# Holding small matmuls to the dense chunk ahead of them, in a two-layer hybrid encoder

## The chip, the cores and the metric

The kernel runs on one core of a Trainium2 chip. The metric is the time of one execution on the device, in microseconds (us): the median of three runs, with the lowest and the highest beside it. The engines of the core are TensorE (PE, with its weight loads listed apart as PEld), VectorE (DVE), ScalarE (ACT), GpSimd (POOL) and SyncE (SP). SP, ACT and POOL also issue DMA transfers.

## The reference

The model is an encoder of two layers over 1040 positions (16 learned ones in front of 1024) with 1024 channels, in float32. In each layer:

- `h = h + hybrid_mixer(rmsnorm(h))`, where one projection gives q, k, v (4 heads of 128, each through a 3-tap convolution and SiLU), a gate z, the coefficients beta and decay, and the three parts B, C, h of a gated short convolution of 512 channels.
- q and k are normalised to length 1. A gated delta rule runs over the positions forwards and backwards: in each chunk, with K the keys and G the running sum of the log decays,

```
M = strict_lower(beta * K K^T * exp(G_i - G_j));  A = I + M
u, w = solutions of A u = beta v, A w = beta k exp(G)
attn = q K^T * exp(G_i - G_j)
v_new = u - w S;  o = q exp(G) S + attn v_new;  S = S exp(G_last) + k_dec^T v_new
```

- both directions are added, normalised per head, multiplied by silu(z), joined with the short convolution, projected out and added to h.
- `h = h + swiglu(rmsnorm(h))` with an inner width of 2816 (22 row tiles of 128).

A last RMSNorm follows, and the 16 learned positions are dropped.

## The kernel before

Activations lie with channels on the partitions: a row is one tile of 128 channels by 1040 positions, and a full activation is eight rows. Float32 products are made of three matmuls: every operand is split into a rounded part and the rest (`hi`, `lo`), and a product is hi*hi + hi*lo + lo*hi.

`dense` (lines 142 to 169) makes one output row: for each chunk of about 347 (or 512) positions it takes a PSUM bank, issues 3 matmuls for each of the K rows of the input, hands the bank to an evacuation, and then takes one job from each of three lists, `jobs`, `jobs2`, `jobs3`. This is how the work of the delta rule is put among the dense projections: a slot is one chunk of 24 matmuls, and a `None` in a list is an empty slot.

The order on each engine is not that of the source alone. The program is built with a planner that runs a timeline of its own, and puts on each engine, at each moment of that timeline, the ready instruction with the smallest priority number. Numbers grow in source order, unless `at_prio` sets them: `low` (line 723) gives a job's matmuls a place behind the dense matmuls issued so far. `after(ins, prev)` (line 85) adds a dependency, so that `ins` comes behind `prev`. On the chip each engine then runs its list in that order and waits where something is not there yet.

In each layer the steps are, in the order of the source:

1. Input projection of the k rows, then the q rows (`seq`, line 660), convolution and SiLU. `lengths` and `sums` (lines 624 to 658) square them and sum over the channels with small matmuls (L629) into a bank of their own; `normalise` scales k.
2. From the fourth tile on, `jobs2` gets one `chunk_p` (line 467) per chunk of positions, 9 in all. It makes the key product K K^T (L477) in bank "b", transposes the keys (`k_out`, L448), and for each direction loads the decay sums (L481, issued by ScalarE), forms the exponents (L483 on VectorE, L484 on ScalarE), stores them for later (L485) and multiplies product by exponents into `P` (L487). Eight buffers `ptm` hold exponents.
3. `sub_start` and `substitute` invert the 32-blocks of A on VectorE. `invert(d)` (line 553) joins them to blocks of 128 with matmuls: `first` (L576), `second_third` for each half of the 32 (chunk, head) pairs (L588, L589), and three `fourth_fifth` (L610, L612), each with copies on ScalarE (L579, L593, L594, L616, L618) that the next step needs. Direction 0 uses banks "f", direction 1 banks "b". They are put into `jobs3`, direction 0 when the last v tile begins, direction 1 with the third z tile.
4. v, z and the short convolution follow (`sc_tile`, line 763); `chunk_a` makes the query products (L513). The scan over the chunks runs beside the last of these projections.
5. The output projection takes first the short-convolution rows. Their splits `ys` (L950, L951) lie in buffers that held rows 4 to 7 of the projection's input `x`; the third of these rows is loaded (L945) into a buffer that held the low parts of rows 0 to 3, and the residual rows `hr` (L967) into those of rows 0 to 3.
6. While the output projection ends, `early_part(f, q)` (line 1095) makes parts of the first four gate tiles f: the half q = 0 is made of four input rows in one bank, copied out by ScalarE (L1105), and the half q = 1 goes on adding in the same bank. Its matmuls are those of `prod` (L1065, L1068, L1069), and each call is chained behind the last matmul of the call before by `after`.
7. SwiGLU with a seven-product scheme of block sums, and the down projection.

## Time and profile before

| | |
|---|---|
| median of three runs | 2469.58 us (2468.56 to 2469.79) |
| profiled execution | 2473.65 us, span 2471.9 us |
| PE busy | 2448.0 us (99%), 17530 instructions |
| VectorE busy | 1779.7 us (72%) |
| ScalarE busy | 1057.9 us (43%) |
| GpSimd busy | 67.2 us (3%) |
| mean DMA rate | 136 GB/s |

The profile is of one execution. Its page gives each engine's busy time, the chain of work that ended last, and the costliest groups; other views list who waited for whom, the busy time of stretches, and the instructions in order of time. A line such as `PE pf L610 <- ACT b L616: 1.9, 1, 1.9` says that PE, before an instruction of line 610 that writes a bank "f", stood idle until ScalarE had done line 616: 1.9 us in all, once, at the longest 1.9. "issue" stands for a wait that no recorded event ended. A row of the timeline gives the start and the length in us, the engine, the line, the operation, out<-in, the shapes, and in brackets the idle time before it and what ended that. The ends of matmuls are modelled: one of 346 columns is shown as some 0.33 us long while the next starts 0.16 us after it. PE's busy time is therefore no measure of how well it is fed; its waits are. Layer 0 is the time up to about 1250 us, layer 1 the rest.

### The profile page before, as it was taken

Reading aid. Unit: us, or ns where it says so; the run is one execution under the profiler, and the core shown is the slowest. Engines: PE = TensorE matmul, PEld = TensorE weight load, DVE = VectorE, ACT = ScalarE, POOL = GpSimd, SP = SyncE. Lnnn points to the kernel's source line nnn. Section 1 sums busy time; section 2 is a strip of 40 time slices with the busy share of each in tenths; the row PEclk is TensorE's granted clock in tenths of the full one; section 3 lists DMA queues with packets and bytes.
Section 4 is the critical chain, followed back from the end, with each engine's and each line's share of the span. In section 5 each row is a group of like instructions: output and inputs, shape, how many; then the busy total and the mean of one; then the engine's idle time right before and its main releaser. Section 6 shows DMA issues by size and latency. Waiting matters only on the chain.

```text
span 2471.9 us, 44873 instructions
## 1 busy us (share of the span) xinstructions
PE 2448.0 (99%) x17530; PEld 2259.7 (91%) x17530; DVE 1779.7 (72%) x3296; ACT 1057.9 (43%) x1964; POOL 67.2 (3%) x157
## 2 busy tenths in 40 slices
PE   9999999999999999999999999999999999999998
PEld 8999999999999999999999988998988888888887
DVE  6788445759877777878667984447798777678775
ACT  5654333536333333444446643335453333234544
POOL 0130000000000000000000200000000000000002
PEclk9999999999999999999999999999999999999999
DMA  4445344524323322675224443535342233237641
GB/s 133 149 155 169 121 160 133 200 76 133 114 90 115 117 95 87 196 228 162 87 91 148 163 153 123 164 124 205 120 139 97 91 111 116 88 110 251 209 132 69
DMA packets 201321, 335.26 MB, mean 136 GB/s; under 512 B 23404, under 2 KB 88356, under 8 KB 201108
## 3 DMA queue, kind: packets, MB, share of 16 engines
q1 hardware_dynamic: 172996, 293.83, 35.9%
q10 hardware_dynamic: 25936, 34.19, 4.3%
q0 software_dynamic: 2176, 4.36, 0.6%
q8 instruction: 138, 2.26, 0.4%
q14 instruction: 75, 0.61, 0.1%
HBM read 250.31 MB, written 81.99 MB: 134 GB/s over the span
## 4 chain that ended last, share of the span: by engine, by line
PE 92%; DVE 4%; DMA 2%; ACT 1%; issue 1%; SPq 0%; ACTq 0%; DVEq 0%
PE pacc L153 10%; PE pacc L154 10%; PE pacc L155 10%; PE pacc L1069 4%; PE pacc L1065 4%; PE pacc L1068 4%; PE pb L1065 3%; PE pb L1069 3%; PE pb L1068 3%; PE pf L1065 3%; PE pf L1069 3%; PE pf L1068 3%; PE pacc L1492 2%; PE pacc L1489 2%; PE pacc L1491 2%; PE pa L1065 1%
## 5 line engine op out<-in xcount | busy, mean ns | idle before, releaser
L153 PE MATMUL pacc<-a,whi 128*128 128x346 f32 (+1 forms) x800 | 263.0, 329 | 2.3 <-ACT a L950 1.0
L155 PE MATMUL pacc<-a,wlo 128*128 128x346 f32 (+1 forms) x800 | 261.0, 327 | 0.1
L153 PE MATMUL pacc<-b,whi 128*128 128x346 f32 (+2 forms) x672 | 233.7, 348 | 0.0
L155 PE MATMUL pacc<-b,wlo 128*128 128x346 f32 (+2 forms) x672 | 232.1, 347 | 0.0
L154 PE MATMUL pacc<-a,whi 128*128 128x346 f32 (+1 forms) x681 | 223.9, 329 | 0.9 <-DVE a L174 0.6
L154 PE MATMUL pacc<-b,whi 128*128 128x346 f32 (+2 forms) x580 | 200.4, 346 | 0.0
L126 ACT ACTIVATE whi<-raw 128x512 fp32r<-128x512 f32 x166 | 104.6, 631 | 221.0 <-PE pacc L154 178.7
L153 PEld LDWEIGHTS pacc<-a,whi 128*128 128x128 f32 x800 | 151.8, 190 | 5.8 <-ACT a L950 1.8
L127 DVE TENSOR_TENSOR wlo<-raw,whi 128x512 fp32r<-128x512 f32 x166 | 114.2, 688 | 59.1 <-ACT whi L126 52.5
L155 PEld LDWEIGHTS pacc<-a,wlo 128*128 128x128 f32 x800 | 151.8, 190 | 1.7 <-issue 1.0
L153 PEld LDWEIGHTS pacc<-b,whi 128*128 128x128 f32 x672 | 126.8, 189 | 10.3 <-issue 1.9
L155 PEld LDWEIGHTS pacc<-b,wlo 128*128 128x128 f32 x672 | 126.5, 189 | 9.2 <-issue 1.3
L154 PEld LDWEIGHTS pacc<-a,whi 128*128 128x128 f32 x681 | 129.2, 190 | 5.1 <-issue 2.0
L1047 ACT ACTIVATE whi<-rw 128x512 fp32r<-128x512 f32 x92 | 58.0, 634 | 140.7 <-PE pf L1068 39.4
L154 PEld LDWEIGHTS pacc<-b,whi 128*128 128x128 f32 x580 | 109.3, 188 | 6.9 <-issue 0.4
L1047 ACT ACTIVATE b<-rw 128x512 fp32r<-128x512 f32 x64 | 40.0, 632 | 134.5 <-PE pacc L1068 38.0
L1047 ACT ACTIVATE a<-rw 128x512 fp32r<-128x512 f32 x64 | 40.4, 633 | 93.8 <-PE pacc L1068 59.9
L316 DVE TENSOR_TENSOR a<-pacc,rstd 128x346 f32<-128x346 f32 (+2 forms) x59 | 32.6, 553 | 50.4 <-PE pacc L155 50.3
L316 DVE TENSOR_TENSOR b<-pacc,rstd 128x346 f32<-128x346 f32 (+1 forms) x63 | 32.4, 514 | 47.7 <-PE pacc L155 47.5
L1048 DVE TENSOR_TENSOR wlo<-rw,whi 128x512 fp32r<-128x512 f32 x92 | 62.8, 685 | 3.4 <-ACT whi L1047 3.1
L1065 PE MATMUL pacc<-b,whi 128*128 128x260 f32 (+1 forms) x172 | 52.7, 307 | 0.7 <-ACT b L1105 0.7
L1069 PE MATMUL pacc<-b,wlo 128*128 128x260 f32 (+1 forms) x172 | 52.7, 306 | 0.0
(981 smaller groups left out, 7866.3 us busy)
## 6 DMA issues: line engine op xcount, KB each, us to landing
raw<-in_w_in SPq DMA_DIRECT2D x110, 256.0 KB
raw<-in_w_gu SPq DMA_DIRECT2D x104, 256.0 KB
rw<-in_w_gu SPq DMA_DIRECT2D x88, 256.0 KB
rw<-in_w_dn SPq DMA_DIRECT2D x94, 192.0 KB
rec<-vkd SPq DMA_DIRECT2D x61, 256.0 KB
raw<-in_w_out SPq DMA_DIRECT2D x48, 256.0 KB
b<-ad SPq DMA_DIRECT2D x45, 260.0 KB
a<-ad SPq DMA_DIRECT2D x45, 256.0 KB
```

The source lines that it names most:

```text
L126: whi_done[0] = act(out=hi, in_=raw[:, 0:kk, :], func=AF.Copy)
L127: whi_done[1] = tt(out=lo, in0=raw[:, 0:kk, :], in1=hi.bitcast(F32), op=ALU.subtract)
L153: mm(ps[:, :n], wh, xh[:, n0:n1], start=(k == 0), stop=False)
L154: mm(ps[:, :n], wh, xl[:, n0:n1], start=False, stop=False)
L155: mm(ps[:, :n], wl, xh[:, n0:n1], start=False, stop=(k == K - 1))
L316: tt(out=t[:, n0:n1], in0=ps, in1=rstd[:, n0:n1], op=ALU.mult)
L1047: act(out=hi, in_=src, func=AF.Copy)
L1048: tt(out=lo, in0=src, in1=hi.bitcast(F32), op=ALU.subtract)
L1065: one = mm(ps[:, :CW], w[0][:, k, :], th[:, cs], start=first and k == 0, stop=False, skip_group_check=True)
L1068: mm(ps[:, :CW], w[0][:, k, :], tl[:, cs], start=False, stop=False, skip_group_check=True)
L1069: one = mm(ps[:, :CW], w[1][:, k, :], th[:, cs], start=False, stop=stop and k == nk - 1, skip_group_check=True)
L1489: one = mm(ps[:, :CW], wh[:, k, :], th[:, cs], start=st, stop=False, skip_group_check=True)
```

## The change

`dense` notes the last matmul that it issued in `last_mm`. The first matmul of each key product, of each length sum and of each inverse step (of `first`, only its first half) gets a dependency on the matmul noted at that time: the last one of the chunk that was issued just ahead of the job.

The slots move: direction 0's `invert` begins three slots later and has two empty slots between the two halves of `second_third`. The exponents' part of `chunk_p` becomes `chunk_g`, and the slot of chunk c makes its product and then the exponents of chunk c+1; those of chunk 0 take the slot ahead.

The last projection of the last `sc_tile` uses, in its last chunk, rows 4 to 7 of its input before rows 0 to 3. The order of the early products changes from (0,0) (0,1) (1,0) (1,1) (2,0) (2,1) (3,0) (3,1) to (0,0) (1,0) (0,1) (1,1) (2,0) (3,0) (2,1) (3,1).

```diff
-    def dense(ws, xs, chunks, evac, pool=None):
+    last_mm = [None]
+
+    def dense(ws, xs, chunks, evac, pool=None, order=None):
...
-            for k in range(K):
+            ks = order if order and n1 == L else range(K)
+            for i, k in enumerate(ks):
                 (wh, wl), (xh, xl) = ws[k], xs[k]
-                mm(ps[:, :n], wh, xh[:, n0:n1], start=(k == 0), stop=False)
+                mm(ps[:, :n], wh, xh[:, n0:n1], start=(i == 0), stop=False)
                 mm(ps[:, :n], wh, xl[:, n0:n1], start=False, stop=False)
-                mm(ps[:, :n], wl, xh[:, n0:n1], start=False, stop=(k == K - 1))
+                last_mm[0] = mm(ps[:, :n], wl, xh[:, n0:n1], start=False, stop=(i == K - 1))
...
-        def chunk_p(c):
+        def chunk_g(c):
 
             if not Pd:
...
             n, s0 = span(c)
-            kk = bank("b").rearrange("p (h i) -> p h i", h=4)
-            for h in range(H):
-                end = mm(kk[0:n, h, 0:n], KTt[:, h, s0:s0 + n], KTt[:, h, s0:s0 + n], start=True, stop=True)
-            k_out(c, end)
             for d in (dirs0 if c == 0 else (0, 1)):
                 gr = ptm[(2 * c + d) % 8]
                 adma(gr[0:n, :, 0:n], gd[36 * d + 4 * c:36 * d + 4 * c + 4, 0:n].partition_broadcast(n))
...
                 act(out=gr[0:n, :, 0:n], in_=gr[0:n, :, 0:n], func=AF.Exp, scale=-1.0)
                 adma(dtd[c, d].rearrange("p (h i) -> p h i", h=4)[0:n, :, 0:n], gr[0:n, :, 0:n])
+
+        def chunk_p(c):
+
+            n, s0 = span(c)
+            kk = bank("b").rearrange("p (h i) -> p h i", h=4)
+            for h in range(H):
+                end = mm(kk[0:n, h, 0:n], KTt[:, h, s0:s0 + n], KTt[:, h, s0:s0 + n], start=True, stop=True)
+                if h == 0:
+                    after(end, last_mm[0])
+            k_out(c, end)
+            for d in (dirs0 if c == 0 else (0, 1)):
+                gr = ptm[(2 * c + d) % 8]
                 dst = P0[d] if c == 0 else Pv[d][:, 4 * c - 4:4 * c, :]
                 tt(out=dst, in0=kk[0:n, :, 0:n], in1=gr[0:n, :, 0:n], op=ALU.mult)
...
-                                 for q in range(qs.start, qs.stop) for (f, s) in pairs])
+                                 for q in range(qs.start, qs.stop) for (f, s) in pairs][0], qs.start == 0)
...
-                low(lambda: [turn(q) for q in range(qs.start, qs.stop)])
+                    return one
+
+                low(lambda: [turn(q) for q in range(qs.start, qs.stop)][0], True)
...
-                low(lambda: [turns(i) for i in range(n)])
+                low(lambda: [turns(i) for i in range(n)][0], True)
...
-            return [first] + [lambda qs=qs: second_third(qs) for qs in halves] + [lambda a=a, b=b: fourth_fifth(a, b) for a, b in (((0, 1), ()), ((2, 3), (0, 1)), ((), (2, 3)))]
+            return [first, lambda: second_third(halves[0])] + [None] * (2 - 2 * d) + [lambda: second_third(halves[1])] + [lambda a=a, b=b: fourth_fifth(a, b) for a, b in (((0, 1), ()), ((2, 3), (0, 1)), ((), (2, 3)))]
...
-                mm(l2s[which][32 * j:32 * j + 32, :n1 - n0], sel[:, 3 - q:35 - q], sq_[:, n0:n1], start=(q == 0), stop=(q == 3), skip_group_check=True)
+                one = mm(l2s[which][32 * j:32 * j + 32, :n1 - n0], sel[:, 3 - q:35 - q], sq_[:, n0:n1], start=(q == 0), stop=(q == 3), skip_group_check=True)
+                if j == 0:
+                    after(one, last_mm[0])
...
-                jobs2.extend([None, None] + [lambda c=c: chunk_p(c) for c in range(9)])
+                jobs2.extend([None, lambda: chunk_g(0)])
+                jobs2.extend([lambda c=c: (chunk_p(c), chunk_g(c + 1)) for c in range(8)] + [lambda: chunk_p(8)])
...
-        def low(f):
+        def low(f, hold=False):
 
             here = tc.cur_priority
             at_prio(mmp[0])
-            f()
+            one = f()
+            if hold:
+                after(one, last_mm[0])
...
-                jobs3.extend(invert(0))
+                jobs3.extend([None] * 3 + invert(0))
...
-                inproj(18 + 3 * i, times(t2), chunks=ochunks)
+                inproj(18 + 3 * i, times(t2), chunks=ochunks, order=(4, 5, 6, 7, 0, 1, 2, 3))
...
-            for f, q in {5: [(0, 0)], 6: [(0, 1)], 7: [(1, 0)]}.get(m, ()):
+            for f, q in {5: [(0, 0)], 6: [(1, 0)], 7: [(0, 1)]}.get(m, ()):
...
-        for f, q in ((1, 1), (2, 0), (2, 1), (3, 0), (3, 1)):
+        for f, q in ((1, 1), (2, 0), (3, 0), (2, 1), (3, 1)):
```

More of the change, by code (lines that the diff above doesn't have):

```diff
@@ L308, in trunk, with inproj @@
         ochunks = TAIL if last else FULL
-        def inproj(i, evac, pool=None, chunks=FULL):
+        def inproj(i, evac, pool=None, chunks=FULL, order=None):
             ws = pre.pop(i) if i in pre else wload(w_in[l, i], KT)
-            dense(ws, x, chunks, evac, pool)
+            dense(ws, x, chunks, evac, pool, order)
         def to_row(t):
@@ L586, in turn @@
                 def turn(q):
-                    for (f, s) in pairs:
-                        mm(ps[B[f], q - qs.start, :], QS[B[s], q, :], P_[B[s], q, B[s]], start=True, stop=True, skip_group_check=True)
+                    one = [mm(ps[B[f], q - qs.start, :], QS[B[s], q, :], P_[B[s], q, B[s]], start=True, stop=True, skip_group_check=True) for (f, s) in pairs][0]
                     mm(ps[B[s0], q - qs.start, :], P_[B[s0], q, B[s0]], QS[B[s0], q, :], start=True, stop=True, skip_group_check=True)
-                low(lambda: [turn(q) for q in range(qs.start, qs.stop)])
+                    return one
+                low(lambda: [turn(q) for q in range(qs.start, qs.stop)][0], True)
                 for (f, s) in pairs:
@@ L607, in turns @@
                 def turns(i):
+                    out = []
                     for q in range(8):
                         if q4s:
-                            mm(pss[i][S_, q, :], P_[F_, 8 * q4s[i] + q, S_], X64[F_, 8 * q4s[i] + q, :], start=True, stop=True, skip_group_check=True)
+                            out.append(mm(pss[i][S_, q, :], P_[F_, 8 * q4s[i] + q, S_], X64[F_, 8 * q4s[i] + q, :], start=True, stop=True, skip_group_check=True))
                         if q5s:
-                            mm(pss[i][F_, q, :], X64[S_, 8 * q5s[i] + q, :], P_[S_, 8 * q5s[i] + q, S_], start=True, stop=True, skip_group_check=True)
-                low(lambda: [turns(i) for i in range(n)])
+                            out.append(mm(pss[i][F_, q, :], X64[S_, 8 * q5s[i] + q, :], P_[S_, 8 * q5s[i] + q, S_], start=True, stop=True, skip_group_check=True))
+                    return out[0]
+                low(lambda: [turns(i) for i in range(n)][0], True)
                 for i, q4 in enumerate(q4s):
```

## The prediction

> **What bounds the kernel now.** I read the page first, then the list of what TensorE waited for, then the timeline around each wait.

> ```profile
> span 2471.9 us, 44873 instructions
> ...
> PE 92%; DVE 4%; DMA 2%; ACT 1%; issue 1%; SPq 0%; ACTq 0%; DVEq 0%
> ```

> TensorE (PE) carries 92% of the chain that ended last. What the change can win is time in which PE stands still, and what it can lose is new time of that kind. All of PE's idle stretches that touch the change are in one short list (engine and line, what was waited for, us in total, times, longest):

> ```profile
> PE pf L610 <- ACT b L616: 1.9, 1, 1.9
> PE pf L588 <- issue: 1.8, 1, 1.8
> PE pb L477 <- DVE P L487: 1.5, 1, 1.5
> ...
> PE pacc L153 <- ACT a L950: 1.0, 2, 0.6
> ...
> PE pa L1065 <- ACT c L1105: 0.8, 1, 0.8
> ...
> PE pacc L1065 <- ACT b L1105: 0.7, 1, 0.7
> PE pf L589 <- issue: 0.7, 1, 0.7
> PE pf L1065 <- ACT b L1105: 0.7, 1, 0.7
> ...
> PE pb L1065 <- ACT b L1105: 0.4, 1, 0.4
> ...
> PE pa L448 <- ACT kt L450: 0.4, 1, 0.4
> PE pacc L154 <- DVE a L951: 0.3, 1, 0.3
> ```

> They add up to 10.2 us, 0.4% of the span: that is nearly the whole prize. The rest of the list is of the kernel's first microseconds, its last ones and the first sums, which the change leaves alone. The next rows are stretches, the last of them one dense chunk (window, its length, PE busy and instructions, clock, DMA share, GB/s):

> ```profile
> 210.68:213.70 3.02, 2.34 (x193) 1.00 0.57 180
> 278.24:279.38 1.14, 1.14 (x98) 1.00 0.00 0
> ...
> 237.41:241.31 3.90, 3.90 (x28) 1.00 0.70 242
> ```

> A dense chunk of 24 matmuls takes 3.90 us (the last row; four of its 28 are neighbours). So one slot of the job lists, a chunk, is worth 3.9 us of cover.

> **The change, part by part.** The sum is made against the profiled execution's own time, 2473.65 us (span 2471.9). The three timed runs have a median of 2469.58, 4.1 us lower, and I take the difference over unchanged. 0.2% of it is 4.9 us, about what a measurement can tell from no change.

> *Inverse steps of direction 0.* Their six steps are moved to later slots and each is held behind the last matmul of the chunk ahead of its slot. What each issues goes along: matmuls, ScalarE copies and three VectorE instructions per half, no DMA; nothing passes SyncE's or GpSimd's queue. The steps now:

> ```profile
> 207.74 0.59 ACT L579 ACTIVATE b<-pf 32x512 f32<-32x512 f32 x1
> 208.36 1.19 ACT L579 ACTIVATE b<-pf 32x512 f32<-32x512 f32 x2
> ...
> 216.41 1.14 PE L610 MATMUL pf<-b,P 64*64 64x64 f32 x16
> 217.83 1.14 PE L610 MATMUL pf<-b,P 64*64 64x64 f32 x16
> ...
> 224.05 0.27 PE L610 MATMUL pf<-b,P 64*64 64x64 f32 x1 [1.92 <-ACT b L616]
> ```

> The row at 224.05 is the fifth step put two dense matmuls into a chunk while its ScalarE copy is not there; PE stands for 1.92 us. In the new order that step waits behind the whole chunk, 22 matmuls or 3.6 us further on, and the copy is done. I take −1.9; the ends are 0 (another step is late in its place) and −1.9. The fourth step stands in two pieces around one dense matmul (216.41, 217.83); held, it is one piece. The gap between the pieces is 0.28 us, and with the like in the other direction's first step I take −0.6 (ends 0 and −0.8).

> *The two halves of the second step* are put two slots apart for direction 0. Now they run together, 192 matmuls, and PE stops in the middle:

> ```profile
> 212.06 0.20 PE L588 MATMUL pf<-P,b 32*32 32x32 f32 x2
> 212.94 0.18 PE L589 MATMUL pf<-b,P 32*32 32x32 f32 x1 [0.68 <-issue]
> ...
> q8 instruction: 3, 0.05, 1.4%
> ...
> q8 instruction: 2, 0.03, 1.3%
> ```

> In the stretch table the pair takes 3.02 us; one half of the other direction, alone between chunks, takes 1.14. So 3.02 − 2 × 1.14 = 0.74 us are lost here and 1.8 in layer 1 (the "issue" row), 2.5 in all. The two queue rows are of 205 to 220 us and of 276 to 286: instruction blocks are fetched at both places, and only where two halves consume them at once, with other DMA running (share 0.57), does PE run dry. Whether the halves really come apart depends on when the first is ready:

> ```profile
> 209.48 0.38 PE L513 MATMUL pb<-b,b 128*128 128x128 f32 x2
> ```

> Its copies end at 208.33 (207.74 + 0.59), inside the chunk behind which this row stands, and the second half is held to the end of that same chunk. Ready one chunk earlier they are apart, else they are only some matmuls apart. I take half, −1.2; the ends are 0 and −2.5.

> [...]

> *Early products.* The two halves (q = 0 and 1) of one row tile use the same bank, and the second must wait until ScalarE has copied the first out. Those are the four rows L1065 <- L1105: 0.8 + 0.7 + 0.7 + 0.4 = 2.6 us. In the new order another product (or an out-projection tile) lies between them, 24 matmuls of 0.12 us (rows below) or 2.9 us, longer than any of those waits. The same loads and splits are issued, in another order on SyncE's queue. −2.6; the ends are −2.6 and +0.8, one such wait by a bank now held longer.

> *Length sums and key products.* The query length sums are one job; now its parts run as early as each row is there:

> ```profile
> 127.93 1.08 PE L629 MATMUL pf<-sq,sel 128*32 128x260 f32 x16
> ...
> 153.39 0.65 PE L629 MATMUL pf<-sq,sel 128*32 128x260 f32 x8
> ...
> 1366.44 0.62 PE L629 MATMUL pf<-sq,sel 128*32 128x260 f32 x2
> ...
> 1391.61 0.65 PE L629 MATMUL pf<-sq,sel 128*32 128x260 f32 x8
> ```

> These are the first and the last visit of four in each layer. A visit of 8 takes 0.65 us and one of 16 takes 1.08, so merging two saves 0.22. Held behind the job's chunk, which ends shortly before the fourth visit, the first three merge: 2 × 0.22 in each layer, and some half chunk less broken up; I take −1.0 (ends 0 and −1.5). The key products' hold binds nothing: each is held to a chunk that has long been done when its rows arrive.

> *Decay exponents one slot ahead.* ScalarE's DMA issues (one load and one store for each chunk and direction) and its exponentials move past one chunk's evacuation:

> ```profile
> 82.22 0.24 ACT L484 ACTIVATE ptm<-ptm 16x64 f32<-16x64 f32 x1
> ...
> 94.34 0.64 ACT L484 ACTIVATE ptm<-ptm 128x512 f32<-128x512 f32 x1 [0.46 <-DVE ptm L483]
> 112.75 0.33 ACTq L481 DMA_DIRECT2D ptm<-gd  x1
> ...
> 129.68 1.14 DVE L483 SCALAR_TENSOR_TENSOR ptm<-ptm,nGb,off 128x128 f32<-128x128 f32 x4 [2.04 <-DMA ptm<-gd]
> ```

> Eight exponents, all that the buffers hold, are done by 95 us, long before the products; the ninth load, at 112.75, waits for a buffer that a product frees. So the lead is there already. The 1.5 us (L477 <- L487) come from the last row: VectorE waits 2.04 us for such a load, and the product that frees the bank is behind it. I take 0, with −1.9 (the waits of L477 and L448) and +1.5 (one more such wait) as ends.

> *Late rows.* In the last chunk of the last input projection the rows 4 to 7 are used first. Their buffers, which the rows for the output projection take, come free 12 matmuls earlier, those of rows 0 to 3 later; into the latter go the third row and eight residual loads of 520 KB on SyncE's queue:

> ```profile
> 473.88 0.38 SPq L945 DMA_DIRECT2D a<-yd  x1
> ...
> 477.99 0.86 ACT L950 ACTIVATE a<-b 128x348 fp32r<-128x348 f32 x2
> ...
> 1698.68 0.32 SPq L945 DMA_DIRECT2D b<-yd  x1
> ...
> 1704.25 1.14 ACT L950 ACTIVATE b<-a 128x512 fp32r<-128x512 f32 x2
> ```

> The splits, first at 477.99, can start about 2 us earlier; the third row's load, now at 473.88, then starts at the projection's end, no later than 477.99: at most 4.1 us later, and in layer 1 5.6 (1704.25 − 1698.68). What PE waits there now is 1.0 + 0.3 us. Gain and loss are of one size, so 0; the ends are −1.3 and +9.7 (4.1 + 5.6, with nothing to fill them).

> *The holds themselves.* The early products are chained by such holds already, and the first matmul after one starts on time:

> ```profile
> 601.94 0.29 PE L1069 MATMUL pb<-a,wlo 128*128 128x260 f32 x1
> 602.06 0.28 PE L1065 MATMUL pa<-b,whi 128*128 128x260 f32 x1
> ```

> 0.12 us, the usual step: 0. At worst each of 24 inverse holds waits out the matmul ahead, 0.28 us less the step of 0.12: +3.8.

> Sum: −1.9 − 0.6 − 1.2 − 2.6 − 1.0 = −7.3, so 2466.3 for a profiled execution and 2462.3 for the median.

> **Rivals.**
> 1. *The inverse's waits only move.* ScalarE's copies come as late at the new places and the halves stay together: −1.9 and −1.2 fall away, −4.2 is left, 2465.4, no measurable change. For it: both halves are ready inside one chunk. Against it: direction 1, at such places already, has no wait in the list.
> 2. *The third row is late.* The output projection stands for its load: −7.3 + 9.7 = +2.4, 2472.0, no change. Against it: scan matmuls lie there to fill in.
> 3. *Slower: VectorE stands for the exponents' loads.* Place: the products of chunks 4 to 8 in both layers. Each pair of exponents now follows straight behind the products of the chunk before; where its load is late, VectorE stops, the bank is not freed and PE stops as at L477. Ten chunks at 1.5 us are +15: 2477.3. It decides from 12.2 us in all, 1.2 a chunk. For it: the 2.04 us. Against it: only one of ten shows it now.

> **How the numbers follow.** Forecast 0.60; rival 1 0.16; rival 2 0.08; rival 3 0.16. Faster 0.60, same 0.24, slower 0.16. The time is the forecast's, 2462.3. Its own range goes down to −12.5 with the lower ends of inverse, halves, products and sums (−1.9 − 0.8 − 2.5 − 2.6 − 1.5 = −9.3) and of the other two (−1.9 − 1.3), 2457; I go to 2455 for what PE loses between matmuls and the list does not show. The upper end takes in rivals 1 and 2 and most of rival 3: 2476.

> **What would show it.** In the list of PE's waits: no L610 <- L616, no L1065 <- L1105, and the two "issue" rows gone or shorter; L629 for the queries in two visits instead of four; each inverse step of direction 0 in one piece at a chunk's end. The L950 row tells of the late rows, L477 <- L487 of the exponents. I am wrong if new rows of over 1 us stand in that list, above all L477, or L153 for the third row.

## The result and the profile after

The changed kernel takes 2465.12 us (median of 22 runs), the kernel before 2469.45 us (22 runs beside them). The ratio is 0.9985, with a 95% interval of 0.9978 to 0.9991: 4.3 us or 0.17% faster by the medians, and 0.15% by the ratio, at the edge of what can be told from no change. The runs of one kernel lie within 0.5% of each other, but for one of 7159.99 us (late rows undone, below), which is left out of that kernel's ratio. The profiled execution of the changed kernel took 2464.69 us, its span is 2462.9 us, 9.0 us shorter than the span of before.

In the changed kernel the lines are numbered anew: `dense` is L156 to L158, the key product L491, the products with the exponents L498, the inverse steps L587 to L624, the early products L1083 to L1087 with their weights' splits L1065 (ScalarE) and L1066 (VectorE), the copies out of their bank L1123, the splits of the short-convolution rows L968.

What PE waited for in the changed kernel (engine and line, what was waited for, us in total, times, longest):

```profile
PE pb L491 <- DVE P L498: 1.6, 3, 0.8
PE pa L753 <- ACT b L765: 1.3, 1, 1.3
PE pa L451 <- ACT kt L453: 1.2, 2, 0.8
...
PE pf L1087 <- DVE wlo L1066: 0.7, 1, 0.7
PE pa L1087 <- DVE wlo L1066: 0.7, 1, 0.7
...
PE pf L1083 <- ACT b L1065: 0.6, 1, 0.6
PE pa L1083 <- ACT b L1065: 0.5, 1, 0.5
...
PE pb L1087 <- DVE wlo L1066: 0.4, 1, 0.4
PE pacc L156 <- ACT a L968: 0.2, 1, 0.2
...
PE pa L1087 <- DVE b L1066: 0.2, 1, 0.2
```

The inverse's wait for its own copy and both "issue" rows are gone, as forecast. Gone too are the four waits of the early products for the copies out of their bank; but six waits for the splits of weights (L1065, L1066) stand in their place, 0.7 + 0.7 + 0.6 + 0.5 + 0.4 + 0.2 = 3.1 us against 2.6 before: the two of 0.7 in the early products of layer 0, the other four in layer 1 in the regular products right behind the early ones. The waits for the short-convolution rows, 1.3 us before, are 0.2. A new wait of 1.3 us is that of a transpose (L753) for a copy on ScalarE, in the middle of the inverse.

The list doesn't hold all of the difference. In the trace of before the granted clock falls four times to half, each time for 3.41 us. Two of these stretches, each with the one ahead of it (window, its length, busy time and instructions of PE, PEld, DVE, ACT and POOL, granted clock, DMA share, GB/s):

```profile
478.37:481.78 3.41, 2.29 (x11) 1.43 (x10) 3.41 (x9) 3.41 (x10) 0.00 (x0) 1.00 0.98 370
481.78:485.20 3.42, 3.12 (x12) 2.82 (x12) 3.42 (x9) 3.42 (x12) 0.00 (x0) 0.50 1.03 398
...
1451.17:1454.58 3.41, 1.67 (x158) 1.55 (x148) 3.31 (x11) 1.05 (x1) 0.00 (x0) 1.00 0.46 142
1454.58:1457.99 3.41, 3.39 (x36) 3.33 (x37) 3.27 (x9) 3.30 (x7) 0.00 (x0) 0.50 0.84 244
```

The seventh column is the clock. In the windows ahead PE stood for 1.12 and 1.74 us (the late rows' waits, the "issue" stop of layer 1); in the windows behind, it worked at 0.50 (matmuls of 348 columns start 0.29 us apart there, at 482.84 and 483.13 us, against 0.16 at 1.00), by estimate up to 3.41 × 0.5 = 1.71 us beside the wait itself. What it did cost is less: kernels below that have the same waits and no such fall are 0.7 us shorter over each of the two stretches. The other two falls, at 10.7 and 58.5 us, lie in the first products and sums, of which the change only holds the length sums of the k rows; in the traces below falls at 55 to 58 us come with that hold and without it. In the changed kernel's trace the clock doesn't fall before the last 12 us, where it falls in every trace. At its turn to the output projection:

```profile
470.00:473.40 3.40, 3.40 (x25) 3.40 (x24) 3.40 (x9) 3.40 (x15) 0.00 (x0) 1.00 0.67 200
473.40:476.80 3.40, 3.18 (x19) 2.44 (x18) 3.40 (x10) 2.96 (x11) 0.00 (x0) 1.00 1.02 409
```

The main matmuls (`dense` and the products) are the same in number and order in all these kernels, so the time between the starts of two of them can be compared from trace to trace. In us, for stretches by the count of such matmuls (start: the first 240; keys: up to 720; inverse: up to 1440; turn: 1920 to 2400; early: 2640 to 3120; in layer 1 keys and inverse 8160 to 9600, turn 9840 to 10560, early 10560 to 11040):

| kernel | start | keys 0 | inverse 0 | turn 0 | early 0 | keys, inverse 1 | turn 1 | early 1 |
|---|---|---|---|---|---|---|---|---|
| before | 58.56 | 97.09 | 158.67 | 94.66 | 60.65 | 323.64 | 149.90 | 110.78 |
| changed | 54.35 | 96.12 | 156.91 | 91.91 | 60.63 | 323.07 | 149.30 | 111.08 |
| late rows alone | 54.29 | 95.78 | 156.86 | 91.95 | 60.57 | 322.96 | 149.10 | 111.78 |
| inverse alone | 54.33 | 99.34 | 156.79 | 93.93 | 61.82 | 322.15 | 149.90 | 110.34 |
| late rows undone | 56.19 | 95.06 | 158.46 | 93.94 | 60.66 | 321.79 | 149.96 | 109.83 |
| inverse undone | 54.22 | 96.68 | 165.46 | 91.91 | 62.24 | 325.45 | 149.30 | 111.42 |
| halves together | 56.17 | 95.86 | 160.76 | 91.91 | 63.66 | 324.32 | 149.30 | 112.81 |
| early order undone | 54.33 | 95.67 | 156.91 | 91.91 | 60.42 | 323.26 | 149.29 | 109.87 |
| weights ahead | 54.56 | 95.38 | 156.89 | 93.45 | 61.21 | 323.30 | 149.30 | 111.45 |
| more load buffers | 56.34 | 96.66 | 156.89 | 93.44 | 62.45 | 322.55 | 149.33 | 113.92 |
| keys undone | 57.79 | 96.66 | 156.97 | 93.49 | 60.67 | 321.41 | 149.10 | 111.15 |
| exponents undone | 54.26 | 96.45 | 156.91 | 91.91 | 60.65 | 321.55 | 149.30 | 111.64 |
| early order undone, own bank | 56.32 | 95.46 | 155.99 | 91.91 | 60.62 | 321.79 | 149.10 | 110.04 |

Of the 9.0 us between the two spans 4.2 lie in the start, which is the same work in all of them. It takes 54.2 to 54.6 us in the seven traces without a fall of the clock there, 56.2 to 56.3 in the four with one and 57.8 to 58.6 in the two with two, before among them (in the two kernels made from the kernel before by one edit it takes 54.3). Leaving that out, 4.8 us are left, close to the 4.3 of the medians. The stretches win 6.7 us: 2.75 at the turn of layer 0, 1.76 at the inverse and 0.97 at the keys of layer 0, 0.6 each at the keys and inverse and at the turn of layer 1. They lose 0.3 in the early products of layer 1 and 0.3 in the gate products and the rest, and the trace of the changed kernel is 0.4 us longer ahead of the first main matmul and 0.9 behind the last.

### The profile page after: what moved, and what is told of

Read it like the earlier page. It is cut to its first block, busy times and chain, and to the rows that moved or that the text cites. A ratio compares the mean times of both kernels' runs of the same rounds, so it can differ in the third digit from the quotient of the medians.

```text
span 2462.9 us, 44865 instructions
## 1 busy us (share of the span) xinstructions
PE 2443.2 (99%) x17530; PEld 2256.0 (92%) x17530; DVE 1783.6 (72%) x3296; ACT 1055.9 (43%) x1964; POOL 68.1 (3%) x157
## 5 line engine op out<-in xcount | busy, mean ns | idle before, releaser
L156 PE MATMUL pacc<-a,whi 128*128 128x346 f32 (+1 forms) x800 | 261.8, 328 | 0.4 <-ACT a L968 0.2
L158 PE MATMUL pacc<-a,wlo 128*128 128x346 f32 (+1 forms) x800 | 259.1, 325 | 0.0
L156 PE MATMUL pacc<-b,whi 128*128 128x346 f32 (+2 forms) x672 | 232.9, 347 | 0.0
L158 PE MATMUL pacc<-b,wlo 128*128 128x346 f32 (+2 forms) x672 | 232.0, 347 | 0.0
L156 PEld LDWEIGHTS pacc<-a,whi 128*128 128x128 f32 x800 | 150.8, 189 | 3.6 <-issue 1.1
L158 PEld LDWEIGHTS pacc<-a,wlo 128*128 128x128 f32 x800 | 150.7, 189 | 1.0 <-issue 0.6
L158 PEld LDWEIGHTS pacc<-b,wlo 128*128 128x128 f32 x672 | 126.4, 188 | 10.0 <-issue 1.7
L156 PEld LDWEIGHTS pacc<-b,whi 128*128 128x128 f32 x672 | 126.4, 188 | 9.5 <-issue 1.0
L1065 ACT ACTIVATE whi<-rw 128x512 fp32r<-128x512 f32 x92 | 57.9, 634 | 134.7 <-PE pf L1086 35.8
L1065 ACT ACTIVATE b<-rw 128x512 fp32r<-128x512 f32 x64 | 40.2, 632 | 140.3 <-PE pacc L1086 38.6
L1065 ACT ACTIVATE a<-rw 128x512 fp32r<-128x512 f32 x64 | 40.2, 631 | 102.8 <-PE pacc L1086 62.6
L1066 DVE TENSOR_TENSOR wlo<-rw,whi 128x512 fp32r<-128x512 f32 x92 | 63.0, 686 | 2.9 <-ACT whi L1065 2.2
L1087 PE MATMUL pacc<-b,wlo 128*128 128x260 f32 (+1 forms) x172 | 52.7, 306 | 0.0
```

The costliest lines, as they stand in the source:

```text
L156: mm(ps[:, :n], wh, xh[:, n0:n1], start=(i == 0), stop=False)
L158: last_mm[0] = mm(ps[:, :n], wl, xh[:, n0:n1], start=False, stop=(i == K - 1))
L1065: act(out=hi, in_=src, func=AF.Copy)
L1066: tt(out=lo, in0=src, in1=hi.bitcast(F32), op=ALU.subtract)
L1087: one = mm(ps[:, :CW], w[1][:, k, :], th[:, cs], start=False, stop=stop and k == nk - 1, skip_group_check=True)
```

## Experiments

The kernels were timed in several sessions, with the kernel before beside them in each; its medians there run from 2469.45 to 2472.37 us. So a difference of some 2 us between the medians of two sessions tells nothing. Each kernel also has one trace, and the planner lays out everything behind an edit anew, so a trace can differ in places that the edit doesn't touch.

### The late rows, alone and undone

The first kernel is the kernel before with this edit alone; the second is the changed kernel without it.

```diff
-                inproj(18 + 3 * i, times(t2), chunks=ochunks)
+                inproj(18 + 3 * i, times(t2), chunks=ochunks, order=(4, 5, 6, 7, 0, 1, 2, 3))
```

> The kernel before with the late rows alone (rows 4 to 7 first in the last chunk of the last input projection). Theory C (clock): the two waits of PE at this place (1.0 and 0.3 us) cost more than they last, because in the trace of before the granted clock falls to 0.5 for 3.41 us right behind them, which is 1.71 us more. So the waits and the fall of the clock at 480 us are gone, the stretch of layer 0 is 2 to 3 us shorter, and the median is 2466.5 to 2468. Rival (prediction): 0, 2469.5, a new wait for the third row's load takes the place.

> The changed kernel with rows 0 to 7 in their old order in the last chunk of the last input projection. T: the late rows carry the largest share, 2.75 us in layer 0 and 0.6 in layer 1, so the stretch at the turn to the output projection is longer by that, waits of PE before the out projection for the splits of the short-convolution rows come back (about 1.3 us in the list), and the median is 2468.4. R (the prediction): the part is worth 0, 2465.1; what differs at the turn between the two traces is the order in which scan matmuls fell there.

Alone: 2466.46 us against 2470.95 of before, ratio 0.9986 (0.9978 to 0.9995), 4.5 us faster by the medians. Undone: 2467.10, ratio to before 0.9991 (0.9982 to 1.0000), so 2.0 us over the changed kernel. Of PE's waits with the late rows alone the first two rows are the stops in the second inverse step, the third is the one left at the turn (lines of that kernel; L951 is the split):

```profile
PE pf L589 <- issue: 1.9, 1, 1.9
...
PE pf L590 <- issue: 0.8, 1, 0.8
...
PE pacc L154 <- ACT a L951: 0.5, 1, 0.5
```

and at the turn with the late rows undone:

```profile
PE pacc L156 <- ACT a L968: 1.1, 2, 0.6
...
PE pacc L157 <- DMA rec<-vkd: 0.4, 1, 0.4
```

In the table the turn of layer 0 takes 91.9 us in every kernel with the late rows but three in which it takes 93.4 to 93.5 (in two of these the clock falls at 495 and 501 us with nothing to be seen ahead of it, in the third a scan matmul waits 0.9 us), and 93.9 without them where no fall follows, 94.7 in before where one does. In layer 1 it is 149.1 to 149.3 with and 149.9 to 150.0 without. So the part is worth 2.0 us in layer 0, 2.75 with the fall, and 0.6 to 0.8 in layer 1. The prediction's 0 is out. The clock theory forecast the size, but not for the reason it gave: 2.0 of the 2.75 us are there in traces without the fall, and the fall itself is worth 0.7. Most of the 2.0 are the waits themselves, which the list shows too short. Its idle time begins at the modelled end of the matmul ahead, some 0.33 us behind that one's start, while the next matmul could have started 0.16 us behind it; three waits of 1.4 us in the list so become some 2 us, against some 0.4 left with the late rows. In layer 1 what goes is a wait of a scan matmul for VectorE (L842), which the prediction hadn't named; in before:

```profile
PE pb L842 <- DVE S L886: 0.4, 1, 0.4
```

T's 2468.4 for the kernel with the late rows undone was too high: the size of 2.75 us had the fall in it.

What the prediction feared, the third row's load, came and cost almost nothing; in the changed kernel (SyncE's load, ScalarE's split, the first out-projection matmul that waits):

```profile
470.93 0.33 SPq L963 DMA_DIRECT2D a<-yd  x1
```

```profile
474.47 1.26 ACT L968 ACTIVATE a<-a 128x348 fp32r<-128x348 f32 x3 [0.44 <-DMA a<-yd]
```

```profile
475.02 1.19 PE L156 MATMUL pacc<-a,whi 128*128 128x348 f32 x3 [0.22 <-ACT a L968]
```

ScalarE waits 0.44 us for the row and PE 0.22 for ScalarE; between the load and that wait PE has other matmuls, of the projections and, at 472.79 us, eight of the scan.

### The inverse, alone and undone

Alone on the kernel before (holds, slots, halves apart), and undone in the changed kernel:

```diff
-                jobs3.extend(invert(0))
+                jobs3.extend([None] * 3 + invert(0))
...
-            return [first] + [lambda qs=qs: second_third(qs) for qs in halves] + [...]
+            return [first, lambda: second_third(halves[0])] + [None] * (2 - 2 * d) + [lambda: second_third(halves[1])] + [...]
...
+            if hold:
+                after(one, last_mm[0])
```

> The kernel before with the inverse's edits alone (holds, three slots later, two empty slots between the halves). Theory C: the wait of 1.9 us and the stops of 0.7 and 1.8 us go, and with the second stop a fall of the clock for 3.41 us, 1.71 us; a transpose waits 1.25 us instead: -4 to -5 us, 2465. Rival I (the parts depend on each other): the inverse's edits only avoid a harm that the new key slots would do, so alone they bring -1 to +1, 2469.

> The changed kernel with the inverse steps as before: no holds, old slots, the two halves of the second step in neighbouring slots. T: in layer 0 the wait of 1.9 us for the copy is back and the stop of about 0.7 us in the middle of 192 small matmuls, while the new wait of 1.25 us of a transpose for ScalarE's copy goes; in layer 1 the stop of about 1.8 us is back: in all +2.5 to +3.5 us, median 2468. Rival A (the prediction as on record): +3.7, and no transpose wait goes, 2468.8. Rival B (the stops have nothing to do with two halves being together): the waits fall where they like, and the sum is -0.5 to +1.

Alone: 2466.84 us against 2470.95, ratio 0.9989 (0.9980 to 0.9997), 4.1 us faster by the medians and 2.7 by the ratio; rival I's −1 to +1 lies at the edge of the interval. Undone: 2480.78, ratio 1.0052 (1.0039 to 1.0065), 15.7 us slower than the changed kernel, nearly four times what the part is worth alone; T, rival A and rival B had all expected at most 3.7. The stretches of the undone kernel in layer 0, two pairs of windows:

```profile
204.09:207.51 3.42, 1.50 (x140) 1.38 (x132) 3.08 (x11) 2.92 (x5) 0.00 (x0) 1.00 0.57 205
207.51:210.92 3.41, 3.41 (x52) 2.97 (x46) 2.25 (x7) 2.45 (x5) 0.00 (x0) 0.50 0.16 41
227.99:231.40 3.41, 1.32 (x8) 1.32 (x9) 3.14 (x11) 0.00 (x0) 0.00 (x0) 1.00 0.14 25
231.40:234.81 3.41, 3.41 (x16) 3.41 (x15) 3.41 (x3) 0.00 (x0) 0.00 (x0) 0.50 0.29 96
```

two rows of its list of waits, and one of ScalarE's timeline:

```profile
PE pacc L158 <- DVE wlo L127: 2.6, 2, 2.3
...
PE pf L598 <- issue: 1.9, 1, 1.9
```

```profile
226.03 0.59 ACT L631 ACTIVATE P<-pf 64x512 f32<-64x512 f32 x1 [6.10 <-DVE Tm L560]
```

With the new key slots the inverse's input is ready inside a chunk; without holds all its steps then run in one place (192 matmuls of the second step, then five pieces of the fourth and fifth between 13 dense matmuls). PE stops in their midst and the clock falls. ScalarE then stands 6.1 us for VectorE, which is in the substitution of the other direction (L560), before the last of the inverse's copies, L631; the splits of the next projection's weights are behind it, PE waits 2.3 us for one at 230 us, and a second fall follows. The stretch of layer 0 is 8.6 us longer, that of layer 1 2.4. So the parts hang together: against the trace of before the inverse's edits alone win 1.9 us in layer 0 and 1.5 in layer 1, and with the new key slots leaving them out costs far more. In that sense rival I is half right.

One finding goes against the prediction's first term. In the kernel with the late rows alone the inverse is as before, its instructions stand in the same order, and yet it has no wait for ScalarE's copy, and the stretch takes 156.86 us instead of 158.67. So that wait of 1.9 us isn't there in every execution. Nor is there a fall of the clock at the stop of layer 1 in this trace: its 1.92 us are cut by the border of two windows into 0.61 and 1.31, while the stop of before lies in one window. Set against this trace, the inverse's edits alone win 0.1 us in layer 0 (156.86 to 156.79) and 0.8 in layer 1 (322.96 to 322.15). The stops of 0.8 and 1.9 us are gone there too, but transposes wait instead (lines of the kernel with the inverse alone):

```profile
PE pa L760 <- DVE vm L753: 1.0, 1, 1.0
...
PE pa L760 <- ACT b3f L761: 0.7, 1, 0.7
```

This is less than the medians give, and what makes up the rest stays open.

### The halves together

```diff
-            return [first, lambda: second_third(halves[0])] + [None] * (2 - 2 * d) + [lambda: second_third(halves[1])] + [...]
+            return [first] + [lambda qs=qs: second_third(qs) for qs in halves] + [...]
```

> The changed kernel without the two empty slots between the halves of direction 0's second step; holds and later slots stay. Theory F (the stop comes from 192 small matmuls in a row): in both layers the two halves stand together or a few matmuls apart, PE stops in their midst for 0.7 to 1.9 us with no event behind it, a fall of the clock follows in at least one layer, +3 to +6 us, 2468 to 2471. Rival S (the stop comes from the old slots): no such stop, the median stays at 2465.

2475.79 us, ratio to before 1.0014 (1.0005 to 1.0022): 4.8 us over the median of before, where the changed kernel is 4.3 under it, so some 9 us between them. PE in layer 0 and layer 1:

```profile
206.63 0.28 PE L753 MATMUL pa<-ident,b3f 128*16 128x128 f32 x1 [1.24 <-ACT b L765]
207.98 0.21 PE L598 MATMUL pf<-P,b 32*32 32x32 f32 x2 [0.36 <-issue]
```

```profile
1452.93 0.21 PE L598 MATMUL pf<-P,a 32*32 32x32 f32 x1 [1.09 <-issue]
```

The stops are back. Over all traces: where the two halves of direction 0 stand together or with one transpose between them (before, late rows alone, inverse undone, halves together, two layers each) PE stops in all eight places, for 0.36 to 1.92 us; where more than that lies between them, if only four transposes, it never does. So the stop belongs to the run of 192 small matmuls with their loads.

That it is the fetch of instructions, as the prediction argued, the traces bear out. The page of every kernel has the same row of the queue that brings PE's instructions (packets, MB, share):

```profile
q8 instruction: 138, 2.26, 0.4%
```

A packet is 16384 bytes. PE has some 35,330 instructions (matmuls, weight loads and the few semaphore instructions between them), so a packet holds 256 of them (35,330 / 138). In all eight places PE stops behind the same count of instructions, 3265 in layer 0 and 23745 in layer 1. Both are 193 more than a multiple of 256, 12 and 92 packets. And in all eight it goes on 1.36 to 1.62 us after the 12th or the 92nd packet has landed. No other such border, in any of the fourteen traces, is reached less than 1.75 us after its packet; with the halves apart that of the 12th is reached 1.9 us after it or later.

Theory F holds for the stops, but its sum was too small. Beside 3.9 us in the inverse of layer 0 (with two windows at half clock, one behind the other) and 1.3 in layer 1, the early products take 3.0 and 1.7 us longer, some 370 us behind the edit: the order of the splits on VectorE there came out differently. This is the planner's doing, and the loss is none of the halves' own.

### The early products: old order, weights ahead, more buffers

```diff
-            for f, q in {5: [(0, 0)], 6: [(1, 0)], 7: [(0, 1)]}.get(m, ()):
+            for f, q in {5: [(0, 0)], 6: [(0, 1)], 7: [(1, 0)]}.get(m, ()):
...
-        for f, q in ((1, 1), (2, 0), (3, 0), (2, 1), (3, 1)):
+        for f, q in ((1, 1), (2, 0), (2, 1), (3, 0), (3, 1)):
```

> The changed kernel with the old order of the early products. My theory now (T): that part brought nothing, because the four waits of 2.6 us for ScalarE's copies out of the bank only became waits of 3.1 us for the splits of the weights on VectorE and ScalarE. So from the first early matmul to the first matmul of the regular gate products this kernel is -0.6 to 0 us against the changed kernel in each layer, the waits behind the copies (about 2.6 us) are back, those behind the weights' splits are gone or mostly gone, and the median is 2464 to 2465.5. The prediction's own theory (R): the part is worth 2.6 us, so this kernel needs about 2467.7, and the same stretch is 2.6 us longer.

2461.98 us, ratio to before 0.9974 (0.9965 to 0.9983): 3.1 us faster than the changed kernel by the medians, 2.7 by the ratios. PE's waits in the early products are those of the copies again, 0.8 + 0.7 + 0.4 = 1.9 us, and none for a split is left, in the regular products neither:

```profile
PE pa L1083 <- ACT c L1123: 0.8, 1, 0.8
PE pacc L1083 <- ACT b L1123: 0.7, 1, 0.7
...
PE pb L1083 <- ACT b L1123: 0.4, 1, 0.4
```

The stretches are 0.2 us shorter in layer 0 and 1.2 in layer 1, and the gate products behind them 0.2 (576.40 against 576.63 us in all kernels but one with the new order, 576.55). The 1.2 need not all be the order's: with the late rows undone, and the new order, that stretch is 109.83 too. T was right in kind; by the medians its size is too small, and where the rest lies stays open (1.4 us of the 3.3 between the two spans lie behind the last main matmul). Why the splits are late was tried twice, both times with the new order. First, two of the weights put ahead in the source:

```diff
+        early_w(1, 1)
+        early_w(2, 0)
         for k in (0, 2):
             t_split(T["T2"], X1, 1, k)
```

> The changed kernel with the loads and splits of the weights of two early products, (1,1) and (2,0), put ahead of the splits of the sums T2 to T4 in the source. Theory W: in the new order the early products wait for nothing but their weights' splits, which stand on VectorE behind splits of 1.26 us each; ahead of them, most of the 3.1 us of such waits goes, and the median is 2462 to 2463.5, as good as the old order of the early products or better. Rival: the loads then hold the two load buffers, the regular products' weights come late instead, and the median stays at 2465.

2465.32 us, ratio to before 0.9980 (0.9971 to 0.9988), as the changed kernel. The splits come no earlier: a load waits for one of two buffers, which the split ahead frees, so the place in the source changes nothing. The median is the rival's, its reason isn't what the trace shows. Then the same with every second load in one of the five small buffers:

```diff
-            A = raw4("raw")
+            A = raw4("ck2" if (f + q) % 2 else "raw")
```

> The changed kernel (new order of the early products) with two of the early weights ahead in the source, as in the run before, and every second early load in one of the five small buffers that the scan used, instead of the two load buffers. Theory B (buffers): the splits were late because a load waits for one of two buffers and takes 2.5 to 3 us; with more buffers the splits stand ready, the waits of 3.1 us behind them fall to under 1 us, and the median is 2462 to 2463. Rival V (VectorE): the splits stand in VectorE's queue behind splits of 1.26 us in an order fixed when the program is built; the waits stay at 2.5 to 3.5 us, 2465.

2470.23 us, ratio 1.0001 (0.9993 to 1.0010): all of the gain is lost. In the early products themselves no wait for a split is left and those of layer 0 gain 2.3 us (matmuls 2640 to 2880), so with more buffers the splits come in time. The regular products behind them then lose 4.1 us (2880 to 3120), and in layer 1 2.8 in all:

```profile
PE pa L1083 <- ACT b L1065: 2.6, 1, 2.6
...
PE pb L1083 <- ACT a L1065: 1.1, 1, 1.1
PE pb L1087 <- DVE a L1066: 1.1, 1, 1.1
```

These wait for the weights of the first regular rows, whose loads use the small buffers too and are now late; behind two of them the clock falls (608 and 1830 us). Theory B holds for the waits that go and fails for the sum: the wait moved once more. Rival V isn't out, since more buffers change the order on VectorE too. In the changed kernel ScalarE had its half of the two late splits of layer 0 done at 584.2 and 595.1 us, and VectorE, busy until then with the splits of the sums and other work, took up its half at 586.72 and 597.14; and the next load starts right behind such a split (587.46), when its buffer is free. The first of the two splits, on ScalarE and on VectorE:

```profile
583.61 0.62 ACT L1065 ACTIVATE whi<-raw 128x512 fp32r<-128x512 f32 x1
```

```profile
586.72 0.71 DVE L1066 TENSOR_TENSOR wlo<-raw,whi 128x512 fp32r<-128x512 f32 x1
```

So the two buffers and VectorE's order hold each other up, and no run takes them apart.

### Key products, exponents and length sums

The changed kernel with all of these as before, and with the exponents alone as before:

```diff
-                jobs2.extend([None, lambda: chunk_g(0)])
-                jobs2.extend([lambda c=c: (chunk_p(c), chunk_g(c + 1)) for c in range(8)] + [lambda: chunk_p(8)])
+                jobs2.extend([None, None] + [lambda c=c: chunk_p(c) for c in range(9)])
...
             k_out(c, end)
+            chunk_g(c)
```

> The changed kernel with key products, exponents and length sums as before: no holds, exponents in the slot of their own chunk. T: what the merged visits and the shorter wait for the product win is lost again in the new waits for the transposed keys' copy (0.4 us in layer 0, 0.8 in layer 1) and for the products (1.2 and 0.4): together +1.0 us in layer 0 and -1 to +0.1 in layer 1, median 2465 to 2466. R (the prediction): +1.0 from the sums in all, 2466.1. Rival C: the exponents one slot ahead are what makes the waits for the keys' copy, so both of those waits go to zero here.

> The changed kernel with the decay exponents back in the slot of their own chunk; holds of key products and length sums stay. The prediction priced this part at 0 (ends -1.9 and +1.5). Theory E: of the 2.3 us that undoing exponents and holds together cost, the exponents carry most, since PE's longest wait for the products is then 1.6 us and not 0.8: 2466 to 2467. Rival H: the holds carry it, so this kernel is at 2465 and only the row of PE waiting for the products changes.

All undone: 2467.46 us, ratio to before 0.9990 (0.9980 to 0.9999), 2.3 us over the changed kernel by the medians and 1.2 by the ratios; T's 2465 to 2466 and R's 2466.1 are both too low, by less than can be told. Exponents alone undone: 2466.44, ratio 0.9986 (0.9976 to 0.9996); against 0.9985 of the changed kernel nothing can be told. In layer 0 the keys' stretch takes 95.86 us on average over the eight kernels with all the new parts (95.06 to 96.68) and 97.22 over the four with the old ones (95.78 to 99.34); in layer 1 keys and inverse take 322.6 over six kernels with all new parts, 321.8 over the two with old keys and the new inverse, 321.55 with the exponents alone undone. So the part wins about 1.4 us in layer 0 and gives back about 0.8 in layer 1, with as much scatter from one trace to the next: the longest of the four, 99.34, is the only one with a fall of the clock there (129 us), and without it the win is 0.7. Rival C is out: with all undone the waits for the keys' copy are gone, but with the exponents alone undone PE still waits 0.7 us for it, so not the exponents make them. Theory E and rival H stay undecided.

### Stalls made on purpose

The changed kernel with a stall of PE in 12 gate rows of each layer, and nothing left out:

```diff
+                if 6 <= f < 18:
+                    n = (16, 256, 512, 1024)[f % 4]
+                    stall = act(out=ss[:, o0:o0 + n], in_=ss[:, o0:o0 + n], func=AF.Copy)
+                    after(stall, p1_end[0])
-                prod(ps["c", j], W["S1"], T["T1"], j, True)
+                prod(ps["c", j], W["S1"], T["T1"], j, True, prev=stall)
```

> The changed kernel with 24 stalls made on purpose, one in each of 12 gate rows of each layer: the first matmul of the fifth product waits for a copy on ScalarE of 16, 256, 512 or 1024 columns of a row onto itself, which starts behind the product ahead (a copy of 512 takes 0.63 us elsewhere). Around them PE does nothing but matmuls of 260 or 512 columns. Theory C (clock): a stall costs more than it lasts. Behind some of the long ones (about 1 us and more) the granted clock falls to 0.5 for 3.41 us, 1.71 us each, behind none of the short ones; with 6 or more falls the kernel is 10 us longer than the sum of its waits. Rival N: the falls in the other traces belong to runs of small matmuls, not to standing, so there is no fall here and the kernel is longer by the sum of the 24 waits alone, some 20 to 30 us.

2556.07 us, ratio 1.0347 (1.0326 to 1.0368), 91 us more than the changed kernel. The waits are longer than meant (up to 4.1 us, ScalarE had other work queued) and come to 59 us; behind them stand eleven windows of 3.41 us at half clock in the gate rows, 18.8 us; of the rest, 13 us, 8.4 are what the list leaves out at these 52 waits, 0.16 us each, because the ends of matmuls are modelled. Two stalls, each with its windows on the grid of 3.41 us on which the falls lie:

```profile
749.29:752.71 3.42, 1.02 (x8) 1.02 (x9) 3.42 (x6) 0.65 (x2) 0.00 (x0) 1.00 0.00 0
752.71:756.12 3.41, 3.41 (x18) 3.41 (x18) 2.07 (x3) 0.00 (x0) 0.00 (x0) 0.50 0.66 249
```

```profile
769.78:773.19 3.41, 2.46 (x21) 2.26 (x19) 2.56 (x5) 1.41 (x3) 0.00 (x0) 1.00 0.00 0
773.19:776.60 3.41, 2.11 (x17) 2.12 (x18) 3.38 (x5) 0.42 (x1) 0.00 (x0) 1.00 0.29 75
776.60:780.02 3.42, 3.42 (x31) 3.42 (x30) 1.74 (x4) 1.85 (x4) 0.00 (x0) 1.00 0.84 303
```

The first stall, 2.5 us, lies in one window: PE stands 2.39 us of it, and the next window runs at 0.50. The second, 2.24 us, is cut by the border at 773.19 into 0.95 and 1.30, and nothing follows. Over the gate rows, of the windows at full clock in which PE stood 0.9 to 1.5 us none of ten was followed by a fall; of those with 1.88 to 2.81 us nine of ten were. Theory C holds and rival N is out: standing alone is enough.

### A bank of its own

The changed kernel with the old early order, and one transpose taken out of the shared bank:

```diff
-            ps = pa()
+            ps = bank("b") if c0 == 0 else pa()
```

> The changed kernel with the old order of the early products, and the transpose of the first 16 positions of v in a bank b instead of the one bank a. Theory: that transpose waits 1.25 us for ScalarE to copy the four transposes ahead of it out of bank a; with another bank the wait is gone, and so is the chance that the granted clock falls behind it. The median is 1 to 2 us under that of the changed kernel with the old early order alone (2461.98), 2460 to 2461. Rival: the four transposes behind it wait for the same copy instead, the wait only moves, 2462; or the query products, whose banks are also b, wait for the copy out of the shared bank, 2462 to 2463.

2462.51 us against 2472.37 of before, ratio 0.9958 (0.9944 to 0.9972). The wait of L753 is gone; the inverse waits 0.5 us for a copy of its own instead:

```profile
PE pf L622 <- ACT b L605: 0.5, 1, 0.5
```

By the trace the inverse of layer 0 is 0.9 us shorter (156.91 to 155.99) and the stretch of layer 1 1.5. The median is 0.5 us above that of the kernel with the early order alone undone; the ratios to the runs beside them, 0.9958 and 0.9974, point the other way, and their intervals overlap. So whether the theory's 1 to 2 us or the rival's none came can't be told. Both beat the kernel before, and by their medians the changed one.

## Why the prediction was right, and where it was wrong

The forecast was −7.3 us and the range 2455 to 2476 us; measured is −4.3 and 2465.12. The direction is right, and two terms of the sum were wrong with opposite signs.

- *The profiled execution against the median.* The prediction carried the 4.1 us between the two over to the changed kernel, whose profiled execution then lies 0.4 us under its median. The 4.1 belonged to the one execution of before: of the 9.0 us between the spans 4.2 are the start, with its two falls of the clock. The sum itself rightly took nothing from them.
- *Inverse's wait (−1.9).* The row is gone, as forecast. As a price it was mis-sized: the wait wasn't there in another trace with the inverse as before, and 1.25 us of a new wait (L753), a transpose's, came in the same place, which the prediction had not named. In the changed kernel:

```profile
205.41 0.28 PE L753 MATMUL pa<-ident,b3f 128*16 128x128 f32 x1 [1.25 <-ACT b L765]
```

- *Steps in one piece (−0.6).* As forecast. The fourth step in the changed kernel is one row of 32, and over the inverse of layer 0 the starts behind a change to the fourth and fifth steps take 1.36 us instead of 1.93:

```profile
215.34 2.08 PE L622 MATMUL pf<-b,P 64*64 64x64 f32 x32
```

- *Halves apart (−1.2, half of 2.5).* Both stops are gone, so the rows of 2.5 us came in whole. The mechanism, instructions fetched too late for 192 small matmuls in a row, was right, as the packets' times show: PE goes on 1.36 to 1.62 us after the 12th or the 92nd has landed. What it brings to the sum is less sure: 5.1 us by the halves put together again (with two windows at half clock), 0.9 in both layers by the inverse alone against the late rows alone, where transposes wait instead.
- *Early products (−2.6).* Wrong. The step that failed is "24 matmuls of 0.12 us or 2.9 us, longer than any of those waits": it looked at the bank alone. The splits of the early weights and of the first regular ones behind them, whose loads share two buffers and which stand on VectorE among other splits, were late next, 3.1 us of waits, and the part costs up to 1.6 us by the traces and 3.1 by the medians. The upper end, +0.8, was too low.
- *Length sums (−1.0).* The visits merge as said, to three and not to two in each layer:

```profile
146.00 1.08 PE L642 MATMUL pf<-sq,sel 128*32 128x260 f32 x16
153.06 0.65 PE L642 MATMUL pf<-sq,sel 128*32 128x260 f32 x8
154.15 0.65 PE L642 MATMUL pf<-sq,sel 128*32 128x260 f32 x8
```

  With the key products and exponents it comes to about −1.4 and +0.8. "The key products' hold binds nothing" can't be told apart from this.
- *Decay exponents (0).* Not to be told from 0 in time; rival 3's long waits at the products didn't come, the longest is 0.8 us.
- *Late rows (0).* Wrong. The step that failed is "gain and loss are of one size": the loss, up to 9.7 us, came to 0.2, because scan matmuls and others fill in, as rival 2's "against" had said; the gain was 2.0 to 2.75 us in layer 0 and 0.6 to 0.8 in layer 1, more than the 1.3 us of its waits, since the list shows each wait some 0.16 us too short and leaves out the fall and layer 1's scan matmul.
- *Rivals.* Rival 1 gives 2465.4, close to the measured time. Its reason is half borne out: the halves do come apart, but a transpose waits in the inverse's place. And the early products, which it leaves at −2.6, brought a loss; so the nearness of its time is partly luck.

What all terms lacked is the clock. Each stall was priced at its own length, though the profile of before showed four falls. Two of them lie behind stalls that the change takes away, and by the traces are worth 0.7 us each; the other two make the 4.2 us of the start, by chance of the execution. By the medians the late rows alone (−4.5), the inverse alone (−4.1) and the early products (+3.1) come to −5.5, with some 2 us of uncertainty on each; by the ratios (−3.5, −2.7, +2.7) they come to −3.5, and the whole to −3.7. That such parts may be added is not shown, and the inverse undone speaks against it.

## What to carry to other kernels

A stall that goes is worth what is late next: before pricing it, look at every input of the waiting instruction (bank, weights, buffers), not only at the one that the list names. Look at the granted clock behind each stall: here nine of ten windows in which PE stood 1.88 to 2.81 us among large matmuls were followed by one of 3.41 us at 0.50, by estimate (3.41 × 0.5) up to 1.7 us more. And price from several executions where the prize is a few tenths of a per cent, since single rows, among them one of 1.9 us here, come and go.
